# A dense SwiGLU layer whose first three column groups multiply the un-normalised residual

## The chip, the cores and the metric

The kernel runs on one NeuronCore of one Trainium2 chip, as one program in one launch. The metric is the device time of one execution, in microseconds (us); lower is better. The core has five engines with a queue each: TensorE (PE, the matmuls), VectorE (DVE), ScalarE (ACT), GpSimdE (POOL) and SyncE (SP, which here only issues transfers). Work on one engine runs in the order of its queue; engines wait for each other through semaphores. SBUF is the on-chip memory of 128 partitions, PSUM the accumulators that TensorE writes and the other engines read.

## The reference

Two trunk layers over 768 tokens (512 latent, 256 context), width 1024. Each layer adds the output projection of four token mixers to the residual stream, and then a channel mix. Layer 0 has a dense SwiGLU, layer 1 a mixture of experts (MoE). What matters here is the end of layer 0's mixers and its channel mix:

```python
x_lat = x_lat + g1 * (jnp.concatenate([hg_l, rw_l, sw_l, ml_l], axis=-1) @ w_out[l])
h2 = rms_norm(x_lat, norm2_g[l]) * (1.0 + sc2) + sh2          # x * rsqrt(mean(x*x)+eps) * g
x_lat = x_lat + g2 * swiglu(h2, w1, w3, w2)                   # (silu(h2@w1) * (h2@w3)) @ w2
# the context tokens likewise, with csc2, csh2, cg1, cg2 in place of sc2, sh2, g1, g2
```

All of it is float32. The factor rsqrt(mean(x*x)+eps) is one number per token, the scale and shift one number per channel and kind of token (latent or context).

## The kernel before, in words

**Layout.** Activations are stored with channels on the partitions: the residual stream is eight tiles `s.x[m]` of 128 channels x 768 tokens (`xm` in the trace). The tokens are handled in two segments, `SEG`: 512 latent and 256 context ones. A float32 product is made of three matmuls in a reduced format: both factors are split into a rounded part and a remainder (`hi`, `lo`), and `mm3` issues hi x hi (L272), lo x hi (L273) and hi x lo (L274). So a weight column group of 128 columns costs 8 k-tiles x 3 matmuls x 2 segments = 48 matmuls. A weight tile comes by a transfer from SP's queue (`load_split`, L264, `raww`), ScalarE rounds it (L259, `hiw`), VectorE or GpSimdE forms the remainder (L260, `low`).

**End of the mixers.** In `mixers` the output projection runs over m = 0 to 7, one group of 128 output channels each. Behind each product `residual` (L1291, two VectorE instructions) adds it to the stream, and `sumsq` adds the squares of the new tile to `acc` (ScalarE L475, GpSimdE L476; for m = 7 VectorE L476, by segments). m = 7 is multiplied segment by segment (`gemm_last`).

**The norm.** `norm_rs` (L481 to L496) turns `acc` into the tokens' factors: matmuls with a column of ones (L487), square root on ScalarE (L489), reciprocal on VectorE (L490), transposes that spread the factors over the partitions (L492), first for the 512 latent tokens and then for the 256 context tokens. Where a tile `rs` is given they are copied out of PSUM (L495). `norm` (L498 to L512) makes, per k-tile and segment, nt = x * A * rs (VectorE L510), the rounded hhi = nt + shift (ScalarE L511) and the remainder hlo (VectorE L512): 32 VectorE and 16 ScalarE instructions for all eight k-tiles.

**The dense layer.** `ffn` (L1542) loads the first three column groups, (0,0), (0,1) and (1,0) (hidden block f, matrix w1 or w3), then does the norm, then multiplies these three together with k outermost (`gemm_cols`), so that they can follow the norm from k-tile to k-tile. Group (1,1) follows alone; then the hidden blocks go on, two groups each, with Silu on ScalarE (L1567), the product on VectorE (L1568) and a split into `gh`, `gl`. Between (1,1) and (2,0) TensorE makes 16 small transposes for the next layer's modulation (L319, in four PSUM groups, copied out at L320 by ScalarE), and VectorE multiplies it (L456). After each of three passes over the hidden blocks the w2 products are added to the stream. The last pass ends in the input norm of layer 1, which uses the same `norm_rs` with `rs` given.

**What sets the order.** The program is written in the order above; a scheduler then places the instructions on each engine's queue and the tiles in SBUF. Pools on the left side of SBUF are stacked; `fh` (hhi and hlo, 48 KB of each partition), `fg` (gh, gl) and `fw` (weights and scratch of the dense layer) lie on each other; while the output projection runs, its own weights and scratch (`ow`, `ox`) lie on the left as well. A transfer into a tile waits for the last reader of whatever lay there before, and SP's queue holds everything behind it. PSUM holds four tiles `big` of 1024 columns.

Of the kernel before, what the change touches and what calls it, by code (L numbers as in the profile page):

```python
# [11 lines left out]
F32 = mybir.dt.float32  # L12
F32R = mybir.dt.float32r
# [3 lines left out]
AF = mybir.ActivationFunctionType  # L17
OP = mybir.AluOpType
AX = mybir.AxisListType
PSUM = bass.MemoryType.PSUM  # L20
# [3 lines left out]
T = LAT + CTX  # L24
KT = D // 128
# [197 lines left out]
class Ker:  # L223
# [1074 lines left out]
    def mixers(s, l, last, xsrc):  # L1298
# [6 lines left out]
        with ExitStack() as wx, ExitStack() as hx:  # L1305
# [160 lines left out]
            with ExitStack() as ox:  # L1466
# [50 lines left out]
                if last:  # L1517
                    s.moe_open()
                else:
                    s.rest = s.ada_rest(s.fx.enter_context(s.pool("fa", side="right")), lambda: s.big())  # L1520
                with s.pool("ox") as wp, s.pool("po", 1, PSUM) as s.pp:
                    s.nbig = 2 if last else 4
                    if last:
                        s.moe_begin(l, wp)
                    for m in range(KT):
                        if m >= 2:
                            load(m)
                            ps = s.big()
                            s.gemm_last(m, ps, ws[m], act, [x for x in SEG if x[0] < nq])
                            if last:  # L1530
                                s.moe_add(l, m, ps, xos[m], s.ow)
                            else:
                                s.residual(s.mods[l][:, 16:24], m, ps, nq, xos[m])
                        if last:
                            s.moe_x(m, wp)
                        else:
                            s.sumsq(m, nq, wp)
                    if last:
                        s.moe_route(wp)


    def ffn(s, l):  # L1542
        E, V, S = s.E, s.V, s.S
        with s.pool("fh") as hh, s.pool("pf", 1, PSUM) as s.pp:
            hhi = hh.tile([128, KT, T], F32R, name="hhi")
            hlo = hh.tile([128, KT, T], F32R, name="hlo")
            with s.pool("fg") as gp, s.pool("fw") as wp:
                def load(f, u):

# [1 line left out]
                first, early = [(0, 0), (0, 1), (1, 0)], [(1, 1), (2, 0)]  # L1551
                loaded = [load(*x) for x in first]
                s.adaw = lambda: wp.tile([128, KT, 128], F32, name="raww", bufs=4).rearrange("p a b -> p (a b)")
                s.norm(l, s.mod2, 0, 8, P_N2, wp, s.norm_rs(wp, None), hhi, hlo, range(KT))

                def up(cols, loaded=None):
                    c = [(s.big(), w, SEG) for w in loaded or [load(*x) for x in cols]]
                    s.gemm_cols(c, lambda k: (hhi[:, k], hlo[:, k]))
                    return [x[0] for x in c]
                pss = up(first, loaded)  # L1560
                for f0, nf in ((0, 8), (8, 7), (15, 7)):
                    gs = []
                    for f in range(f0, f0 + nf):
                        while len(pss) < 2:
                            pss += up([(f, len(pss))])
                        t = wp.tile([128, T], F32, name="fs", bufs=2)
                        S.activation(t, pss[0][:, :T], AF.Silu)  # L1567
                        V.tensor_mul(t, t, pss[1][:, :T])  # L1568
                        a = gp.tile([128, T], F32R, name=f"gh{f - f0}")
                        c = gp.tile([128, T], F32R, name=f"gl{f - f0}")  # L1570
                        s.split(a, c, t)
                        gs.append((a, c))
                        for _ in range((0 if f == 0 else 1 if f == 8 else 2)):
                            next(s.rest, None)
                        pss = pss[2:]
# [411 lines left out]
```

## Time and profile before

| | |
|---|---|
| median of 3 runs | 2631.07 us (2624.13 to 2632.36) |
| profiled execution | 2628.14 us, its span 2626.2 us, 1.94 us outside |
| TensorE busy | 2406.9 us, 92% of the span; mean granted clock 0.967 |
| VectorE, ScalarE, GpSimdE busy | 1588.0, 1233.2, 478.2 us |
| output projection's last matmul starts | 794.95 us |
| first matmul of the dense layer starts | 804.23 us |
| dense layer's last matmul starts | 1363.38 us |

Times within the span count from its start. A busy share is a mean over very different stretches: TensorE works without a pause in most of the dense layer, and stands still in places around the norms. The granted clock is the share of TensorE's full clock that the chip allowed it in a stretch: 1.00 is 2.4 GHz, 0.50 is 1.2 GHz, and a value between is a stretch with some of both.

### The profile page before, as it was taken

How to read it: one execution, taken by the hardware profiler on the slowest of the kernel's cores; microseconds unless marked ns; L12 is line 12 of the kernel's file. 1: busy time of each engine (PE TensorE's matmuls, PEld its weight loads, DVE VectorE, ACT ScalarE, POOL GpSimd, SP SyncE). 2: the span in 40 equal slices, each digit the busy share in tenths (PEclk: the TensorE clock that was granted, in tenths of full speed). 3: DMA queues.
4: the chain of work that ended last, by engine and by line, in shares of the span. 5: the costliest groups of instructions: out<-in, count | busy, mean ns of one | idle time of the engine just before them, and what ended most of it. 6: DMA issues, size and time to landing. Idle time of an engine off the chain costs nothing. (4 is left out here: it accounts for less than half of the span.)

```text
span 2626.2 us, 46769 instructions
## 1 busy us (share of the span) xinstructions
PE 2406.9 (92%) x18379; PEld 1997.7 (76%) x18379; DVE 1588.0 (60%) x2981; ACT 1233.2 (47%) x2347; POOL 478.2 (18%) x613
## 2 busy tenths in 40 slices
PE   6999889879999999999999997888996999999994
PEld 4889666656587888888888786666674898898993
DVE  5573588877525643443236747877745667767765
ACT  4373356646723211212234644664753565656553
POOL 2010455441011000000020005654112000000002
PEclk9999899999999999999999998999997999999997
DMA  6223222221031533333212130001113888888885
GB/s 247 70 84 111 68 71 84 86 82 57 1 125 47 162 113 121 122 115 117 81 61 72 52 114 13 20 16 56 51 48 120 266 268 276 277 260 264 263 272 178
DMA packets 173061, 322.49 MB, mean 123 GB/s; under 512 B 12033, under 2 KB 100865, under 8 KB 172833
## 3 DMA queue, kind: packets, MB, share of 16 engines
q1 hardware_dynamic: 165776, 293.60, 34.9%
q0 software_dynamic: 6480, 23.73, 2.5%
q8 instruction: 146, 2.39, 0.4%
q10 hardware_dynamic: 576, 2.10, 0.2%
q14 instruction: 83, 0.67, 0.1%
HBM read 295.39 MB, written 22.54 MB: 121 GB/s over the span
## 5 line engine op out<-in xcount | busy, mean ns | idle before, releaser
L272 PE MATMUL big<-hhi,hiw 128*128 128x512 f32 (+1 forms) x1504 | 520.6, 347 | 9.8 <-ACT hhi L511 6.1
L273 PE MATMUL big<-hlo,hiw 128*128 128x512 f32 (+1 forms) x1504 | 522.1, 347 | 2.4 <-DVE hlo L512 2.4
L274 PE MATMUL big<-hhi,low 128*128 128x512 f32 (+1 forms) x1504 | 518.4, 345 | 0.9 <-POOL low L260 0.9
L259 ACT CAST hiw<-raww 128x512 fp32r<-128x512 f32 (+3 forms) x208 | 158.7, 769 | 616.3 <-PE big L273 405.2
L272 PEld LDWEIGHTS big<-hhi,hiw 128*128 128x128 f32 x1504 | 285.9, 190 | 53.7 <-ACT hhi L511 7.6
L273 PEld LDWEIGHTS big<-hlo,hiw 128*128 128x128 f32 x1504 | 285.8, 190 | 40.2 <-DVE hlo L512 3.9
L274 PEld LDWEIGHTS big<-hhi,low 128*128 128x128 f32 x1504 | 285.4, 190 | 38.5 <-issue 1.7
L260 DVE TENSOR_TENSOR lom<-rawm,him 128x1024 fp32r<-128x1024 f32 x176 | 215.2, 1225 | 126.3 <-ACT him L259 124.2
L260 DVE TENSOR_TENSOR low<-raww,hiw 128x512 fp32r<-128x512 f32 (+3 forms) x196 | 172.4, 884 | 185.8 <-ACT hiw L259 185.3
L259 ACT CAST him<-rawm 128x1024 fp32r<-128x1024 f32 x176 | 184.3, 1047 | 149.1 <-PE sml L273 64.0
L272 PE MATMUL sml<-xh,him 128*128 128x256 f32 x528 | 152.1, 288 | 0.0
L273 PE MATMUL sml<-xl,him 128*128 128x256 f32 x528 | 149.7, 284 | 0.0
L274 PE MATMUL sml<-xh,lom 128*128 128x256 f32 x528 | 149.7, 283 | 0.0
L260 DVE TENSOR_TENSOR lov<-rawv,hiv 128x1024 fp32r<-128x1024 f32 x88 | 107.6, 1223 | 40.5 <-ACT hiv L259 40.4
L272 PE MATMUL sml<-him,xh 128*128 128x256 f32 x440 | 127.5, 290 | 0.6 <-DVE xl L260 0.6
L273 PE MATMUL sml<-lom,xh 128*128 128x256 f32 x440 | 125.5, 285 | 0.0
L274 PE MATMUL sml<-him,xl 128*128 128x256 f32 x440 | 125.4, 285 | 0.0
L273 PE MATMUL big<-gl,hiw 128*128 128x512 f32 (+1 forms) x352 | 119.6, 340 | 0.0
L272 PE MATMUL big<-gh,hiw 128*128 128x512 f32 (+1 forms) x352 | 119.1, 338 | 0.0
L274 PE MATMUL big<-gh,low 128*128 128x512 f32 (+1 forms) x352 | 118.3, 336 | 0.0
L259 ACT CAST hiv<-rawv 128x1024 fp32r<-128x1024 f32 x88 | 92.4, 1050 | 54.2 <-PE y L274 43.9
L777 POOL TENSOR_TENSOR Gm<-G,mskf 128x256 f32<-128x256 f32 x120 | 97.2, 815 | 81.2 <-PE a L632 77.5
(557 smaller groups left out, 5568.4 us busy)
## 6 DMA issues: line engine op xcount, KB each, us to landing
rawm<-in_m SPq DMA_DIRECT2D x176, 512.0 KB, 5.0
rawv<-in_m SPq DMA_DIRECT2D x88, 512.0 KB, 5.0
raww<-in_w SPq DMA_DIRECT2D x52, 512.0 KB, 3.7
raww<-in_wadt SPq DMA_DIRECT2D x48, 512.0 KB, 3.5
raww<-in_winc SPq DMA_DIRECT2D x92, 256.0 KB, 2.9
wada<-in_wada SPq DMA_DIRECT2D x16, 1024.0 KB, 6.1
raww<-in_wout SPq DMA_DIRECT2D x16, 512.0 KB, 4.4
raww<-in_w SPq DMA_DIRECT2D x16, 448.0 KB, 3.3
```

The costliest lines, as they stand in the source:

```text
L259: s.S.copy(hi, src)
L260: (eng or s.V).tensor_sub(lo, src, hi)
L272: s.E.matmul(out, ah, bh, start=start, stop=False)
L273: s.E.matmul(out, ah, bl, start=False, stop=False)
L274: s.E.matmul(out, al, bh, start=False, stop=stop)
L777: P.tensor_mul(x, G[:, :, 0, :, 0], s.mskf[:, 1 - d, i][:, None, None].to_broadcast(sh))
```

## The change

The tokens' factors do not depend on the channel, so they can be applied behind a product as well as ahead of it: (x * A * rs + shift) @ W = rs * ((x * A) @ W) + shift @ W. The change uses that for the first three column groups.

- A pool `uh` on the right side of SBUF holds `s.uh`, hi and lo of 8 k-tiles x 770 columns. `norm_scale` computes A and puts the shifts of the two kinds of tokens into columns 768 and 769. `scaled(m)`, called behind each `sumsq`, writes x * A, rounded and remainder: 2 ScalarE (L1562) and 2 VectorE instructions (L1563) for each m.
- `ffn` multiplies the three groups from `s.uh` with segments of 512 and 258 columns; only then come `norm_rs` (into `acc`) and `norm`, which writes the normalised hi and lo over the same tiles. The pool `fh` is gone.
- `normed` multiplies each of the three products by the factors in PSUM (L1584) and copies its two shift columns out (L1586, `nb`). They enter as the bias of the Silu (L1608) and as the addend of the product with w3 (L1610).

```diff
--- before.py
+++ after.py
@@ -1517,6 +1517,11 @@
                 if last:
                     s.moe_open()
                 else:
+
+                    uh = s.fx.enter_context(s.pool("uh", side="right"))
+                    s.uh = [uh.tile([128, KT, T + 2], F32R, name=f"u{n}") for n in "hl"]
+                    s.uA = uh.tile([128, KT, 2], F32, name="uA")
+                    s.norm_scale(s.uA)
                     s.rest = s.ada_rest(s.fx.enter_context(s.pool("fa", side="right")), lambda: s.big())
                 with s.pool("ox") as wp, s.pool("po", 1, PSUM) as s.pp:
                     s.nbig = 2 if last else 4
@@ -1535,15 +1540,32 @@
                             s.moe_x(m, wp)
                         else:
                             s.sumsq(m, nq, wp)
+                            s.scaled(m)
                     if last:
                         s.moe_route(wp)
 
 
+    def norm_scale(s, A):
+
+        V = s.V
+        V.scalar_tensor_tensor(A, s.mod2[:, 8:16], 1.0, s.prm[:, 0, P_N2:P_N2 + 8][:, :, None].to_broadcast([128, KT, 2]),
+                               op0=OP.add, op1=OP.mult)
+        hi, lo = (x[:, :, T:] for x in s.uh)
+        V.tensor_copy(hi, s.mod2[:, :8])
+        V.tensor_sub(lo, s.mod2[:, :8], hi)
+
+    def scaled(s, m):
+
+        hi, lo = (x[:, m] for x in s.uh)
+        for v, (o, n) in enumerate(SEG):
+            c = slice(o, o + n)
+            s.S.activation(hi[:, c], s.x[m][:, c], AF.Copy, scale=s.uA[:, m, v:v + 1])
+            s.V.scalar_tensor_tensor(lo[:, c], s.x[m][:, c], s.uA[:, m, v:v + 1], hi[:, c], op0=OP.mult, op1=OP.subtract)
+
     def ffn(s, l):
         E, V, S = s.E, s.V, s.S
-        with s.pool("fh") as hh, s.pool("pf", 1, PSUM) as s.pp:
-            hhi = hh.tile([128, KT, T], F32R, name="hhi")
-            hlo = hh.tile([128, KT, T], F32R, name="hlo")
+        with s.pool("pf", 1, PSUM) as s.pp:
+            hhi, hlo = s.uh
             with s.pool("fg") as gp, s.pool("fw") as wp:
                 def load(f, u):
 
@@ -1551,21 +1573,43 @@
                 first, early = [(0, 0), (0, 1), (1, 0)], [(1, 1), (2, 0)]
                 loaded = [load(*x) for x in first]
                 s.adaw = lambda: wp.tile([128, KT, 128], F32, name="raww", bufs=4).rearrange("p a b -> p (a b)")
-                s.norm(l, s.mod2, 0, 8, P_N2, wp, s.norm_rs(wp, None), hhi, hlo, range(KT))
+
+                useg = (0, LAT), (LAT, CTX + 2)
+                pss = [s.big() for _ in first]
+                s.gemm_cols([(ps, w, useg) for ps, w in zip(pss, loaded)], lambda k: (hhi[:, k], hlo[:, k]))
+                rs = s.acc
+                s.norm_rs(wp, rs)
+
+                def normed(ps):
+                    V.tensor_mul(ps[:, :T], ps[:, :T], rs)
+                    b = wp.tile([128, 2], F32, name="nb", bufs=3)
+                    V.tensor_copy(b, ps[:, T:T + 2])
+                    return b, ps
+                s.norm(l, s.mod2, 0, 8, P_N2, wp, rs, hhi, hlo, range(KT))
 
                 def up(cols, loaded=None):
                     c = [(s.big(), w, SEG) for w in loaded or [load(*x) for x in cols]]
                     s.gemm_cols(c, lambda k: (hhi[:, k], hlo[:, k]))
-                    return [x[0] for x in c]
-                pss = up(first, loaded)
+                    return [(None, x[0]) for x in c]
+
+                pss = [normed(ps) for ps in pss]
                 for f0, nf in ((0, 8), (8, 7), (15, 7)):
                     gs = []
                     for f in range(f0, f0 + nf):
                         while len(pss) < 2:
                             pss += up([(f, len(pss))])
                         t = wp.tile([128, T], F32, name="fs", bufs=2)
-                        S.activation(t, pss[0][:, :T], AF.Silu)
-                        V.tensor_mul(t, t, pss[1][:, :T])
+                        (b1, x1), (b3, x3) = pss[:2]
+                        if b1 is None:
+                            S.activation(t, x1[:, :T], AF.Silu)
+                        for v, (o, n) in enumerate(SEG):
+                            k = slice(o, o + n)
+                            if b1 is not None:
+                                S.activation(t[:, k], x1[:, k], AF.Silu, bias=b1[:, v:v + 1])
+                            if b3 is not None:
+                                V.scalar_tensor_tensor(t[:, k], x3[:, k], b3[:, v:v + 1], t[:, k], op0=OP.add, op1=OP.mult)
+                        if b3 is None:
+                            V.tensor_mul(t, t, x3[:, :T])
                         a = gp.tile([128, T], F32R, name=f"gh{f - f0}")
                         c = gp.tile([128, T], F32R, name=f"gl{f - f0}")
                         s.split(a, c, t)
```

How the queues stand before and after. Names in the rows: `in_w` are the dense layer's weights, `in_wout` the output projection's, `in_wadt` the next layer's modulation, `xo` the old stream for `residual`. SyncE's queue around the last part of the output projection, before:

```order
L264 DMA raww<-in_wout 128x1024 x2
L264 DMA raww<-in_w 128x1024 x4
L451 DMA raww<-in_wadt 128x1024 x2
L264 DMA raww<-in_w 128x1024
L1481 DMA xo<-in_xT 128x768 x2
L264 DMA raww<-in_wout 128x1024 x2
L1481 DMA xo<-in_xT 128x768
```

And after:

```order
L264 DMA raww<-in_wout 128x1024 x2
L1481 DMA xo<-in_xT 128x768 x2
L264 DMA raww<-in_wout 128x1024 x2
L1481 DMA xo<-in_xT 128x768
L264 DMA raww<-in_wout 128x1024
L1481 DMA xo<-in_xT 128x768
L264 DMA raww<-in_wout 128x1024
L1481 DMA xo<-in_xT 128x768 x2
L264 DMA raww<-in_w 128x1024 x4
L451 DMA raww<-in_wadt 128x1024 x2
```

The first five weight tiles of the dense layer have moved from the middle of the output projection's loads to behind the last of them; the tiles that they fill now lie where the output projection's weights and scratch lie, and the first of the five waits for the last matmul of the projection and the last L476.

TensorE's queue from the last matmul of the output projection, before (`big<-hhi,hiw` behind L492 is the product of the first three groups):

```order
L274 MATMUL big<-hhi,low 128x256
L487 MATMUL big<-cst,acc 128x1 x4
L492 MATMUL big<-cst,rstd_8356 128x128 x4
L487 MATMUL big<-cst,acc 128x1 x2
L492 MATMUL big<-cst,rstd_8365 128x128 x2
L272 MATMUL big<-hhi,hiw 128x512 x3
L273 MATMUL big<-hlo,hiw 128x512
```

And after, from the last two matmuls of the three groups; the first of the 144, `L272 MATMUL big<-uh,hiw 128x512`, now stands directly behind the output projection:

```order
L273 MATMUL big<-ul,hiw 128x258
L274 MATMUL big<-uh,low 128x258
L487 MATMUL big<-cst,acc 128x1 x4
L492 MATMUL big<-cst,rstd_8539 128x128 x4
L487 MATMUL big<-cst,acc 128x1 x2
L492 MATMUL big<-cst,rstd_8549 128x128 x2
L272 MATMUL big<-uh,hiw 128x512
L273 MATMUL big<-ul,hiw 128x512
L274 MATMUL big<-uh,low 128x512
```

The factors' matmuls have moved from ahead of the 144 matmuls of the three groups to between them and group (1,1).

VectorE's queue after the change at the end of the norm (before, nothing stands between the last L512 and the first product L1568 there):

```order
L510 SCALAR_TENSOR_TENSOR nt<-xm_68,nA,acc 128x256
L1584 TENSOR_TENSOR big<-big,acc 128x768
L512 SCALAR_TENSOR_TENSOR ul<-nt,mod_95,uh 128x256
L1586 COPY nb<-big 128x2
L1584 TENSOR_TENSOR big<-big,acc 128x768 x2
L1586 COPY nb<-big 128x2 x2
L260 TENSOR_TENSOR low<-raww,hiw 128x1024
L1610 SCALAR_TENSOR_TENSOR fs<-big,nb,fs 128x512
L1610 SCALAR_TENSOR_TENSOR fs<-big,nb,fs 128x256
```

Behind the norm's last instruction the rest of the three groups' post-processing has come in, ahead of what frees their PSUM tiles. At the end of the dense layer SyncE's queue changes too: ten of the loads of layer 1's projection weights (`in_winc`, 128x512) stood between the last loads of `in_w`, and stand now behind the copies of the last stream tiles (`xd<-xm`).

## Rows read from the trace of the kernel before

**Rows 1.** page, part 1: busy us of each engine

```profile
PE 2406.9 (92%) x18379; PEld 1997.7 (76%) x18379; DVE 1588.0 (60%) x2981; ACT 1233.2 (47%) x2347; POOL 478.2 (18%) x613
```

**Rows 2.** three stretches: length, then busy us per engine, PE clock, DMA share

```profile
797.60:804.20 6.60, 3.83 (x18) 3.29 (x18) 2.14 (x6) 1.27 (x4) 0.00 (x0) 0.54 0.01 1
804.20:808.20 4.00, 3.97 (x11) 3.30 (x12) 4.00 (x9) 2.38 (x5) 0.00 (x0) 0.50 0.00 0
808.20:829.60 21.40, 21.40 (x125) 18.79 (x124) 11.71 (x22) 6.38 (x12) 0.00 (x0) 0.99 0.00 1
```

**Rows 3.** the sum over seven stretches from 853 to 1363 us

```profile
sum 510.00, PE 510.00 PEld 447.03 DVE 206.54 ACT 104.42 POOL 16.67; mean PE 72.86 PEld 63.86 DVE 29.51 ACT 14.92 POOL 2.38
```

**Rows 4.** TensorE in time, 794.9 to 842.7: start, length, line, operation, [idle before]

```profile
794.95 0.28 PE L274 MATMUL big<-hhi,low 128*128 128x256 f32 x1
...
797.69 1.38 PE L487 MATMUL big<-cst,acc 128*128 128x1 f32 x8 [2.45 <-DVE acc L476]
...
804.23 0.80 PE L272 MATMUL big<-hhi,hiw 128*128 128x512 f32 x1 [1.59 <-ACT hhi L511]
...
831.43 0.40 PE L272 MATMUL big<-hhi,hiw 128*128 128x512 f32 x1
...
841.01 1.91 PE L319 MATMUL big<-cst,scp 128*128 128x128 f32 x16
842.67 0.48 PE L272 MATMUL big<-hhi,hiw 128*128 128x512 f32 x1
```

**Rows 5.** VectorE in time, 796.8 to 833

```profile
796.85 1.03 DVE L476 TENSOR_TENSOR acc<-acc,sq 128x512 f32<-128x512 f32 x2 [0.44 <-ACT sq L475]
...
802.68 1.80 DVE L510 SCALAR_TENSOR_TENSOR nt<-xm,nA,big 128x512 f32<-128x512 f32 x3 [0.78 <-PE big L492]
...
820.00 0.48 DVE L512 SCALAR_TENSOR_TENSOR hlo<-nt,mod,hhi 128x256 fp32r<-128x256 f32 x1 [0.58 <-ACT hhi L511]
832.62 0.95 DVE L1568 TENSOR_TENSOR fs<-fs,big 128x768 f32<-128x768 f32 x1 [12.13 <-ACT fs L1567]
```

**Rows 6.** SyncE, ScalarE and VectorE in time: the first FFN weights

```profile
727.55 1.75 SPq L264 DMA_DIRECT2D raww<-in_w  x4
...
731.21 1.05 ACT L259 CAST hiw<-raww 128x1024 fp32r<-128x1024 f32 x1 [3.04 <-DMA raww<-in_w]
...
734.87 1.05 ACT L259 CAST hiw<-raww 128x1024 fp32r<-128x1024 f32 x1 [1.20 <-DMA raww<-in_w]
...
732.28 1.23 DVE L260 TENSOR_TENSOR low<-raww,hiw 128x1024 fp32r<-128x1024 f32 x1 [4.49 <-ACT hiw L259]
```

**Rows 7.** VectorE and TensorE at column m = 2

```profile
742.18 2.20 DVE L1291 SCALAR_TENSOR_TENSOR xm<-sc,mod,xo 128x512 f32<-128x512 f32 x4 [5.00 <-PE sc L274]
744.28 2.36 DVE L260 TENSOR_TENSOR low<-raww,hiw 128x1024 fp32r<-128x1024 f32 x2
...
744.52 0.47 PE L272 MATMUL big<-hhi,hiw 128*128 128x512 f32 x1 [2.02 <-DVE xm L1291]
```

**Rows 8.** ScalarE behind the first three columns

```profile
830.48 1.28 ACT L1567 ACT_TABLE_LOAD   x1
...
841.64 1.07 ACT L320 COPY cb<-big 128x512 f32<-128x512 f32 x2 [3.94 <-PE big L319]
```

**Rows 9.** the boundary to layer 1: TensorE, VectorE, SyncE, casts, transfers

```profile
1366.12 1.02 PE L487 MATMUL big<-cst,acc 128*128 128x1 f32 x8 [2.45 <-DVE acc L476]
...
1371.01 0.80 PE L272 MATMUL big<-hhi,hiw 128*128 128x512 f32 x1
...
1369.02 0.75 DVE L510 SCALAR_TENSOR_TENSOR rwr<-xm,nA,rwvt 128x512 f32<-128x512 f32 x1 [1.37 <-ACT rwvt L495]
...
1307.38 8.86 SPq L264 DMA_DIRECT2D raww<-in_winc  x5
...
L259 ACT CAST hiw<-raww 128x512 fp32r<-128x512 f32 x6 | 3.7, 618 | 7.7 <-PE big L273 7.6
...
raww<-in_winc SPq DMA_DIRECT2D x10, 256.0 KB, 3.9
```

## The prediction

> **What bounds the kernel now.** I read the page first, then TensorE's time line around the dense layer, then the other engines' time lines over the same stretch, and last the boundary to layer 1. The page gives TensorE 92% of the span [rows 1], so the question is where TensorE stands still and whether the change fills or makes such places. The table of stretches answers for the body of the dense layer: from 853 to 1363 us TensorE is busy for all of the 510 us [rows 3]. Nothing lost or won ahead of that stretch can be given back or eaten in it; a microsecond at its start is a microsecond at its end.
>
> The place that the change aims at is the norm. The output projection's last matmul starts at 794.95, the first one of the dense layer at 804.23: a hole of 9.0 us in which only the small matmuls of the factors run [rows 4]. The clock follows: 0.54 in the hole, 0.50 for the 4.0 us behind it, then 0.99 [rows 2]. Four us at half speed do two us of work, so the hole costs some 11 us in all. The three groups then run from 804.23 to 831.43, that is 27.2 us, or 25.2 at full clock; 8.4 us for one group. VectorE's norm lies beside them: its 32 instructions take from 802.68 to 820.48, 17.8 us [rows 5], and are through 11 us before the product is. That cover matters most below.
>
> **The change part by part.**
>
> *Weights.* Before, the first weights were issued at 727.55 and rounded from 731.21 on, the third at 734.87 [rows 6], 70 us before use. In the new order of SyncE their loads stand behind the last load of the output projection, into memory that it uses until its last square is added. That addition (L476) ends at 797.88 [rows 5]. It also comes a little later: at m = 2 VectorE's remainder of a weight now stands behind two more instructions (L1563), for which I take half of the 2.20 us of four L1291 of the same sizes, 1.1 us, and TensorE waits at that place as it is [rows 7]; bounds 0 and 2.2. So the loads go out at 799.0. By the intervals of before (3.66 us to the first cast, 7.32 to the third [rows 6]) the first cast starts at 802.6, the first matmul at 803.7; the third remainder starts 1.07 behind its cast, takes 1.23, and is ready at 808.6. With k outermost the three groups need all three weights for their first k-tile. If that waits for the weights alone, the other seven k-tiles (7/8 of 25.2 = 22.0) end at 831; if the clock is at half, the first k-tile takes 6.3 us and they end at 832. I take 832.0 against 831.43: the hole is not filled, but changes its cause, from the norm to the weights. Term: +0.6, bounds -1 and +3. The 32 new instructions of `scaled` otherwise lie beside TensorE's output projection, where VectorE and ScalarE wait for products; the two extra columns of 72 matmuls are under 0.1 us.
>
> *The norm behind the product.* Call the product's end G. In TensorE's new order the factors' matmuls come behind the 144, and group (1,1) behind those. `norm` overwrites what the 144 read, and (1,1) reads what it writes, so the whole pass now stands between them. The factors with `rs` given are in the trace, at the boundary to layer 1: first L487 at 1366.12, first L510 at 1369.02 [rows 9], 2.9 us. Then VectorE's pass, 17.8 us [rows 5], with one L1584 inside it that I price as L1568, 0.95 us for 768 columns out of PSUM [rows 5], and the reciprocal and copy of the second segment, 0.5 us. The last L512 ends at G + 22.2, and (1,1) just behind it, at G + 22.6. Before, (1,1) ended 9.6 us behind the product (841.01 - 831.43 [rows 4]). That is +13.0. Where before three groups of matmuls (27 us) covered the pass, one group of 8.4 us is left to do it.
>
> *What frees PSUM.* The transposes L319 need the tiles of the three products. Behind the last L512 VectorE has two L1584 (1.9), three small copies (0.4), one weight remainder (1.23 [rows 6]) and two L1610 (1.1, as L1291 [rows 7]): 4.6 us. Then the last group of transposes (a quarter of 1.91 [rows 4]) and its copy (half of 1.07 [rows 8]) and (2,0) can start: G + 27.8, where before it started at 842.67, G + 11.2. The whole term from G to (2,0) is +16.6, the 13.0 within it. Bounds: 13 if VectorE's instructions run closer together without an operand in PSUM and the tail lies beside the transposes, 19 if ScalarE's Silus with bias and their table load (1.28 [rows 8]) come last in the tail.
>
> *Clock.* No row shows TensorE behind such a sparse stretch, but the rows of the hole do: half speed after some 7 us that were half idle [rows 2]. In (1,1) half speed would cost little, since a k-tile takes 2.1 us at half and the pass gives one each 2.2. Behind the 5 us of the tail, (2,0) would lose 2 us in its first 4. I take +1.5; bounds 0 and 4.
>
> *The boundary to layer 1.* Ten loads of layer 1's weights went out before the dense layer's end, five of them at 1307.38 [rows 9]. Now they stand behind the last copies of the stream and come in only after the layer's last matmul. A load takes 3.9 us at the median, a cast 0.62 [rows 9]. In ScalarE's and VectorE's new order two or three casts and remainders, and two table loads for the square root, get in between L489, L495 and L510, on a chain that is already the path from 1366.12 to 1371.01 [rows 9]. Two casts and the first table load ahead of the first L510 are 2.5 us, the second table load delays the context tokens further: +3.0; bounds 0 (all of it beside waits) and 5 (two table loads and four casts in a row).
>
> On those table loads a rule speaks for more. The row shows 1.28 us, and ScalarE starts its next instruction 0.01 us behind it, at 831.77 after 830.48 + 1.28 [rows 8]. The Trainium skill (ScalarE: Activation LUTs, "What ACT_TABLE_LOAD costs") adds a drain to each switch and comes to about 2.66 us; by it the boundary would be some 2.8 us dearer. This trace shows no such gap behind the load, so the sum keeps the row.
>
> **The sum.** 0.6 + 16.6 + 1.5 + 3.0 = +21.7 us, against a profiled execution of 2628.14 (span 2626.2 and 1.94 around it): 2649.8. The median of the runs shown is 2.9 above that execution, so by the median it is 2652.8. I predict 2651. The bounds of all terms together are +12 and +31.
>
> **The rivals.**
>
> *A: the product closes the hole.* If the first weights are there (the transfers wait for less than I read from the order, or land beside the last additions), the product starts at 795.2 at full clock and ends at 820.4, 11 us earlier. For it: the order does put the 144 matmuls straight behind the projection, and 76 us before use was time enough so far. Against: SyncE's order, and the reuse of memory. The pass behind it is still paid: -11 + 16.6 + 1.5 makes +7, less or more with the boundary (0 to 3): 2635 to 2641, at the edge of no change.
>
> *B, the other side: the factors leave the path for good.* The mechanism would be that group (1,1) does not wait for the whole pass because VectorE's work for it is done beside TensorE's, as now. Its place is the stretch between the product and (2,0); it decides at 2.2 us for a k-tile on VectorE against 1.05 on TensorE at full clock. If the pass were ahead of TensorE and the hole closed too, the gain is the whole 11 us, minus about 3 us of chain: 2620 to 2623. Against: 17.8 us of work on one engine, and 8.4 us of matmuls left to hide it.
>
> *C: a larger loss.* TensorE's clock stays at half through the sparse 28 us and beyond. The row that speaks for it is the 0.54 and 0.50 around 801 [rows 2]. A k-tile of (1,1) then takes a little more than the pass gives, the transposes and the first groups behind run at half, and the boundary costs its upper bound: +6 for the clock in place of 1.5, +5 in place of 3, +3 for the weights: +31 us, 2660 to 2664. The Trainium skill (TensorE: Matmul & The Clock Gate, "A second HAM failure mode: psum-queue depth-cycling") tells of a kernel in which short idle times between groups of matmuls made the clock swing between its two levels; here (1,1) would have such pauses in front of each k-tile. What the trace of before has of it is the one hole at 797.6.
>
> *D: no effect where it aims, and none elsewhere.* If the pass behind the product lay beside other TensorE work, the time would be unchanged, about 2631 to 2634. TensorE's queue is in order, and nothing stands there that could run meanwhile, so this needs the order not to be what runs.
>
> **How the numbers follow.** The forecast (+12 to +27) has a chance of 0.74, C 0.09, A 0.10, D 0.03, B 0.04. What a measurement of this kernel can tell from no change is about 0.3%, 7.9 us, so up to 2639 counts as the same. A lies half across that edge: faster 0.04 (B), same 0.10 (D, most of A, and a sliver of the forecast's low end), slower 0.86. The range leaves out B, D, half of A and the far end of C: 2637 to 2663.
>
> **What would show it.** Weights: the first `big<-uh,hiw` matmul near 804, with TensorE waiting for ScalarE's cast or VectorE's remainder, and `raww<-in_w` issued near 799. The norm: L487 directly behind the product near 832; (1,1) drawn out over about 20 us with waits for ScalarE's or VectorE's output; (2,0) near 860. Clock: a stretch of 0.5 behind 832, and full clock soon after (2,0). Boundary: layer 1's first `big<-hhi,hiw` about 8 us, not 5, behind its first L487. I would be wrong if the first weights are loaded long before 795, if (1,1) follows the product within 5 us at its old speed, or if TensorE shows idle time in the 510 us that are full now.

## The result, and the profile after

The changed kernel takes 2653.63 us (median of 6 runs, 2650.56 to 2657.03), the kernel before 2630.11 (6 runs, 2624.13 to 2632.36). The ratio is 1.0095, with a 95% interval of 1.0079 to 1.0111: slower by 25 us, 21 to 29 (the two medians differ by 23.5). The forecast was 2651, from a sum of +21.7.

The profiled execution took 2654.09 us with a span of 2652.3, 26.1 more than before. TensorE's time line of the changed kernel, as in [rows 4]:

```profile
799.64 0.28 PE L274 MATMUL big<-hhi,low 128*128 128x256 f32 x1
...
807.77 0.77 PE L272 MATMUL big<-uh,hiw 128*128 128x512 f32 x1 [7.85 <-issue]
...
835.88 0.95 PE L487 MATMUL big<-cst,acc 128*128 128x1 f32 x8
837.40 0.65 PE L492 MATMUL big<-cst,rstd 128*128 128x128 f32 x4 [0.57 <-DVE rstd L490]
838.73 0.61 PE L487 MATMUL big<-cst,acc 128*128 128x1 f32 x4 [0.68 <-ACT acc L495]
840.39 0.69 PE L492 MATMUL big<-cst,rstd 128*128 128x128 f32 x2 [1.06 <-DVE rstd L490]
841.68 0.77 PE L272 MATMUL big<-uh,hiw 128*128 128x512 f32 x1 [0.61 <-DVE acc L495]
...
859.72 0.65 PE L319 MATMUL big<-cst,scp 128*128 128x128 f32 x4 [1.15 <-ACT fs L1608]
861.16 2.82 PE L319 MATMUL big<-cst,scp 128*128 128x128 f32 x12 [0.79 <-ACT fs L1608]
863.63 0.75 PE L272 MATMUL big<-uh,hiw 128*128 128x512 f32 x1
```

The hole behind the output projection is still there (799.64 to 807.77), the three groups follow, and at 835.88 the factors begin, where before group (1,1) began at once. (1,1) starts at 841.68, and (2,0) at 863.63: 27.75 us behind the product's end and not 11.24 [rows 4]. What TensorE waited for from 790 to 870 (engine, line, by whom: us in total, times, longest; `issue` means that the profile shows nothing it waited for):

```profile
PE big L272 <- issue: 7.9, 1, 7.9
PE big L273 <- DVE ul L512: 2.4, 4, 0.9
PE big L319 <- ACT fs L1608: 1.9, 2, 1.1
PE big L492 <- DVE rstd L490: 1.6, 2, 1.1
```

VectorE, SyncE and ScalarE, as in [rows 5, 6, 8]: the last addition, the loads right behind it, the first casts, and the norm pass between the product and (1,1)'s end.

```profile
801.54 1.03 DVE L476 TENSOR_TENSOR acc<-acc,sq 128x512 f32<-128x512 f32 x2 [0.44 <-ACT sq L475]
...
838.71 1.55 DVE L510 SCALAR_TENSOR_TENSOR nt<-xm,nA,acc 128x512 f32<-128x512 f32 x1 [1.36 <-ACT acc L495]
...
857.54 0.47 DVE L512 SCALAR_TENSOR_TENSOR ul<-nt,mod,uh 128x256 fp32r<-128x256 f32 x1
...
802.69 1.75 SPq L264 DMA_DIRECT2D raww<-in_w  x4
...
806.63 2.14 ACT L259 CAST hiw<-raww 128x1024 fp32r<-128x1024 f32 x2 [3.88 <-issue]
...
857.32 1.28 ACT L1608 ACT_TABLE_LOAD   x1
858.62 1.05 ACT L1608 ACTIVATE fs<-big,nb 128x512 f32<-128x512 f32 x2
```

The granted clock over the sparse stretch, as in [rows 2]:

```profile
840.00:845.00 5.00, 3.67 (x9) 2.27 (x10) 4.87 (x11) 3.25 (x5) 0.00 (x0) 0.53 0.37 118
845.00:850.00 5.00, 4.76 (x19) 3.46 (x18) 5.00 (x11) 3.23 (x6) 0.00 (x0) 0.78 0.00 0
850.00:856.00 6.00, 3.93 (x16) 2.45 (x16) 6.00 (x12) 3.48 (x6) 0.00 (x0) 1.00 0.00 0
862.00:866.00 4.00, 4.00 (x22) 3.68 (x21) 3.69 (x6) 3.13 (x5) 0.00 (x0) 0.72 0.41 131
```

It is at half where (1,1) begins (0.53), and back to full (1.00 from 850 to 856) while TensorE still waits in front of each k-tile; behind the tail, around the start of (2,0), it falls once more for a moment (0.72). The boundary to layer 1, as in [rows 9]:

```profile
1388.46 1.02 PE L487 MATMUL big<-cst,acc 128*128 128x1 f32 x8 [2.45 <-DVE acc L476]
...
1396.09 1.63 PE L272 MATMUL big<-hhi,hiw 128*128 128x512 f32 x3
...
1393.56 0.74 DVE L510 SCALAR_TENSOR_TENSOR rwr<-xm,nA,rwvt 128x512 f32<-128x512 f32 x1
...
1390.31 1.28 ACT L921 ACT_TABLE_LOAD   x1
1391.61 0.20 ACT L921 ACTIVATE lb<-lb 128x4 f32<-128x4 f32 x1
...
1393.86 1.28 ACT L489 ACT_TABLE_LOAD   x1
...
1386.04 0.81 SPq L264 DMA_DIRECT2D raww<-in_winc  x2
...
1387.38 13.01 SPq L264 DMA_DIRECT2D raww<-in_winc  x8
```

The loads of `in_winc` start 2.4 us ahead of the first L487, where the first of them started some 60 us ahead of it before; casts and two table loads come in on ScalarE, and the first L510 is 5.1 us behind the first L487 (2.9 before), the first matmul of layer 1 7.6 us (4.9).

### The profile page after: what moved, and what is told of

Read it like the earlier page. It is cut to its first block, busy times and chain, and to the rows that moved or that the text cites. A ratio compares the mean times of both kernels' runs of the same rounds, so it can differ in the third digit from the quotient of the medians.

```text
span 2652.3 us, 46837 instructions
## 1 busy us (share of the span) xinstructions
PE 2416.6 (91%) x18379; PEld 1999.4 (75%) x18379; DVE 1610.5 (61%) x3008; ACT 1248.2 (47%) x2370; POOL 480.6 (18%) x613
## 5 line engine op out<-in xcount | busy, mean ns | idle before, releaser
L272 PE MATMUL big<-hhi,hiw 128*128 128x512 f32 (+1 forms) x800 | 280.6, 352 | 7.3 <-ACT hhi L511 3.5
L273 PE MATMUL big<-hlo,hiw 128*128 128x512 f32 (+1 forms) x800 | 282.0, 353 | 3.1 <-DVE hlo L512 3.1
L274 PE MATMUL big<-hhi,low 128*128 128x512 f32 (+1 forms) x800 | 280.5, 351 | 1.4 <-DVE low L260 1.4
L272 PE MATMUL big<-uh,hiw 128*128 128x512 f32 x704 | 240.9, 342 | 9.0 <-issue 7.9
L273 PE MATMUL big<-ul,hiw 128*128 128x512 f32 x704 | 240.5, 342 | 2.7 <-DVE ul L512 2.4
L274 PE MATMUL big<-uh,low 128*128 128x512 f32 x704 | 239.1, 340 | 0.0
L272 PEld LDWEIGHTS big<-hhi,hiw 128*128 128x128 f32 x800 | 151.7, 190 | 35.3 <-ACT hhi L511 5.6
L273 PEld LDWEIGHTS big<-hlo,hiw 128*128 128x128 f32 x800 | 151.5, 189 | 28.1 <-DVE hlo L512 5.2
L272 PEld LDWEIGHTS big<-uh,hiw 128*128 128x128 f32 x704 | 134.4, 191 | 26.8 <-issue 8.0
L272 PE MATMUL sml<-xh,him 128*128 128x256 f32 x528 | 151.9, 288 | 0.0
L273 PEld LDWEIGHTS big<-ul,hiw 128*128 128x128 f32 x704 | 134.2, 191 | 20.0 <-DVE ul L512 4.5
L260 DVE TENSOR_TENSOR lov<-rawv,hiv 128x1024 fp32r<-128x1024 f32 x88 | 107.6, 1222 | 35.1 <-ACT hiv L259 35.0
L272 PE MATMUL sml<-him,xh 128*128 128x256 f32 x440 | 127.1, 289 | 0.6 <-DVE xl L260 0.6
```

The lines of the kernel that those rows point to most:

```text
L260: (eng or s.V).tensor_sub(lo, src, hi)
L272: s.E.matmul(out, ah, bh, start=start, stop=False)
L273: s.E.matmul(out, ah, bl, start=False, stop=False)
L274: s.E.matmul(out, al, bh, start=False, stop=stop)
```

## The experiments

Times are medians with the ratio to the kernel before, measured beside it on the same chip. The stretches in the table at the end of this section are read from each run's trace.

**1. The factors ahead of the product.**

```diff
-                s.gemm_cols([(ps, w, useg) for ps, w in zip(pss, loaded)], lambda k: (hhi[:, k], hlo[:, k]))
                 rs = s.acc
                 s.norm_rs(wp, rs)
+                s.gemm_cols([(ps, w, useg) for ps, w in zip(pss, loaded)], lambda k: (hhi[:, k], hlo[:, k]))
```

> The changed kernel with one thing moved: the tokens' factors (L487 to L495) are computed ahead of the three groups' product again, so that the in-place norm can follow the product's k-tiles. Theory (the loss is the norm pass standing between the product and group (1,1)): the hole ahead of the product stays, its first matmul near 808, because the weights still come late; the product ends near 836 as in the changed kernel; (2,0) starts 11 to 14 us behind the product's end and not 28; the time falls by 13 to 16 us, to about 2638 to 2640, and is still some 9 us above the kernel before. Rival (the moved memory is the loss, not the order): the time stays near 2653, with the 28 us as they were.

Measured: 2636.78 us, ratio 1.0032 (1.0015 to 1.0048), 17 us less than the changed kernel, a little below the expected range. TensorE, and ScalarE's first two casts:

```profile
796.00 0.28 PE L274 MATMUL big<-hhi,low 128*128 128x256 f32 x1
798.74 1.02 PE L487 MATMUL big<-cst,acc 128*128 128x1 f32 x8 [2.45 <-DVE acc L476]
...
803.56 0.69 PE L492 MATMUL big<-cst,rstd 128*128 128x128 f32 x2 [0.55 <-DVE rstd L490]
804.30 0.80 PE L272 MATMUL big<-uh,hiw 128*128 128x512 f32 x1
...
843.17 1.91 PE L319 MATMUL big<-cst,scp 128*128 128x128 f32 x16
844.83 0.48 PE L272 MATMUL big<-uh,hiw 128*128 128x512 f32 x1
...
803.21 1.98 ACT L259 CAST hiw<-raww 128x1024 fp32r<-128x1024 f32 x2
```

The product starts 8.3 us behind the projection, as late as in the changed kernel, although the factors' whole chain now stands in that hole. The last L492 (803.56 + 0.69) and the first cast end within 0.1 us of each other, so either alone would hold the product about as long. (2,0) comes 48.8 us behind the projection's end, where the changed kernel needs 64.0. (1,1) now starts right behind the product, at 833.45, and (2,0) 11.4 us later. The order was the loss, as the theory had it: 15.3 of the 17 us came back between the product's first matmul and (2,0). The rival of the moved memory alone falls: its memory is where it was.

**2. The raw weights early.**

```diff
-            with s.pool("fg") as gp, s.pool("fw") as wp:
+            with s.pool("fg") as gp, s.pool("fw") as wp, s.pool("fr", side="right") as rp:
...
-                s.adaw = lambda: wp.tile(
+                s.adaw = lambda: rp.tile(
...
+                        sq = [wp.tile([128, T], F32, name="sq")] * 2
...
-                            s.sumsq(m, nq, wp)
+                            s.sumsq(m, nq, sq)
```

(Both calls of `load_split` in the dense layer take `rp` for the raw tile as well.)

> The changed kernel with the raw weight tiles of the dense layer in a pool of their own on the right side of SBUF, in memory that the output projection does not use (its square scratch is one tile in place of two for that), so that their loads go out in the middle of the projection as before. Rounding still has to wait for the projection's end, since the rounded tiles lie in its memory. Theory: the first FFN matmul starts 1.5 to 3 us behind the projection's end in place of 8.1, the product ends 5 to 7 us earlier, the stretch from there to (2,0) is 27 to 28 us as in the changed kernel, layer 1's boundary as in the changed kernel: 2646 to 2649. Rival (the moved memory is the whole loss): the time comes near that of the kernel before, 2630 to 2636. Rival (the hole is the chain of the last addition, not the weights): no change.

Measured: 2647.47 us, ratio 1.0078 (1.005 to 1.0107). The loads went out at 728.51 and the hole shrank from 8.1 to 4.15 us, a little over the expected 1.5 to 3: the three casts stand behind the last tile's squares and scaling on ScalarE (801.81, where the projection's last matmul started at 798.79). The stretch behind the product is the changed kernel's (27.6 us). Both rivals fall: the time is far from that of the kernel before, and the hole shrank although the chain of the last addition was not touched.

```profile
799.96 0.94 ACT L475 ACTIVATE sq<-xm 128x512 f32<-128x512 f32 x2 [4.76 <-DVE xm L1291]
800.80 1.11 ACT L1564 ACTIVATE uh<-xm,uA 128x512 fp32r<-128x512 f32 x2
801.81 2.93 ACT L259 CAST hiw<-raww 128x1024 fp32r<-128x1024 f32 x3
...
802.94 0.77 PE L272 MATMUL big<-uh,hiw 128*128 128x512 f32 x1 [3.87 <-issue]
```

**3. No norm pass at all.**

```diff
-                s.norm(l, s.mod2, 0, 8, P_N2, wp, rs, hhi, hlo, range(KT))
...
-                    c = [(s.big(), w, SEG) for w in loaded or [load(*x) for x in cols]]
+                    c = [(s.big(), w, useg) for w in loaded or [load(*x) for x in cols]]
...
-                    return [(None, x[0]) for x in c]
+                    return [normed(x[0]) for x in c]
```

> The changed kernel without the norm pass: all 44 column groups multiply the un-normalised residual, and each product gets its factors and its shift behind it (one L1584 and one L1586 more for each of the other 41 groups, and two L1610 in place of one product). Theory: behind the three groups' product only the factors' chain is left ahead of (1,1), about 6 us, then its 8.4 us and the transposes: (2,0) 16 to 18 us behind the product in place of 28, the time 10 to 12 us lower, 2641 to 2644; VectorE's 41 x 1.3 = 53 us more lie beside TensorE, which is full from there on. Rival (VectorE becomes the bound in the body of the layer): TensorE shows waits for VectorE between the groups there, and the time does not fall, or rises.

Measured: 2645.86 us, ratio 1.0075 (1.0047 to 1.0103), 2 us above the expected range. The place does what was expected: factors at 831.26, (2,0) at 848.09, 16.8 us and not 27.75. TensorE shows no wait in the body of the layer, so VectorE's additional work is hidden; but the body is 4.2 us longer than before (524.96 and 520.71 us). Of these 1.1 us are there in every trace with the residual's tiles on the right side (last section). The rest goes with the products of this run: 96 matmuls take 17.01 us and not 16.85, which is 3.3 ns more for each of the 48 that have two columns more. At the mean of 0.46 ns per column (16.80 us for 48 x 768 columns) two columns would be 0.9 ns; why they cost more was not tried. The rival of VectorE, waits between the groups, falls.

**4 and 7. The kernel before with the hidden activations at the bottom.**

```diff
-        with s.pool("fh") as hh, s.pool("pf", 1, PSUM) as s.pp:
+        with s.pool("fg") as gp, s.pool("fh") as hh, s.pool("pf", 1, PSUM) as s.pp:
...
-            with s.pool("fg") as gp, s.pool("fw") as wp:
+            with s.pool("fw") as wp:
```

> The kernel before with one thing changed: the tiles of the hidden activations (gh, gl) lie at the bottom of the left side and the normalised residual above them, the other way round than before. This is where gh and gl lie in the changed kernel. Nothing else moves around the first three groups. Theory: the loads of layer 1's first weights wait for the dense layer's last matmul, and the boundary (first L487 to layer 1's first matmul) goes from 4.9 to about 7.6 us, as in the changed kernel: +2.5 to +3, 2633. Rival (the boundary got longer by the later order of the casts alone, or for another reason than memory): no change, 2630.

> The kernel before with the hidden activations at the bottom once more (the fourth run): there the trace showed the boundary 2.7 us longer, and the time was 9.9 us above before, more than its own trace adds up to (3.3 us). Theory (the boundary and the waits for weights behind it are all that changes, the rest was the spread of single executions): +2 to +5. Rival (the layout costs some 10 us, in a place which that trace did not catch): +8 to +12 again, and the trace shows the place.

Measured: 2638.16 us, ratio 1.0043 (1.003 to 1.0056), then 2635.39, ratio 1.0025 (1.0014 to 1.0036). Both traces have the boundary as the changed kernel has it. The second one's:

```profile
1362.64 1.02 PE L487 MATMUL big<-cst,acc 128*128 128x1 f32 x8 [2.46 <-DVE acc L476]
...
1367.55 1.01 PE L487 MATMUL big<-cst,acc 128*128 128x1 f32 x4 [2.67 <-ACT rwvt L495]
...
1370.26 1.65 PE L272 MATMUL big<-hhi,hiw 128*128 128x512 f32 x3
...
1316.96 37.07 SPq L1962 DMA_DIRECT2D xd<-xm  x6
1360.22 0.81 SPq L264 DMA_DIRECT2D raww<-in_winc  x2
...
1361.55 13.02 SPq L264 DMA_DIRECT2D raww<-in_winc  x8
...
PE big L273 <- DVE low L260: 1.6, 2, 1.2
```

From the dense layer's last matmul to layer 1's first are 10.35 us in both (7.63 before), and the layout alone does it: no other edit is in this kernel. But the time rose by 9.9 and 6.7 us, more than these 2.7. Some of the rest is behind the boundary: the later loads also bring waits of TensorE for a weight remainder, in this trace at 1523 and 1530 (the last line). All nine traces with gh and gl low have such waits, 1.2 to 1.8 us in all, and neither trace of the kernel before has one. The stretch from layer 1's first matmul on is 4 us longer in both traces, but that is not shown to be the layout's: with the same layout it is as short as before in the changed kernel and in runs 2 and 5, and long in runs 1, 3, 6 and 9, and the six traces that have it long all came to m = 2 early (table). So by their medians the layout costs these two kernels 4 to 7 us more than the boundary shows, run 7 between the two ranges expected; where, and how much of that the changed kernel pays, stays open.

**5. The losses mended together.** Early raw weights as in run 2, and:

```diff
-                s.gemm_cols([(ps, w, useg) for ps, w in zip(pss, loaded)], lambda k: (hhi[:, k], hlo[:, k]))
-                rs = s.acc
-                s.norm_rs(wp, rs)
+                gc = lambda ks: s.gemm_cols([(ps, w, useg) for ps, w in zip(pss, loaded)], lambda k: (hhi[:, k], hlo[:, k]), ks)
+                gc(range(0, 1))
...
+                gc(range(1, 3))
...
+                gc(range(3, KT))
...
-                            s.scaled(m)
+                            if m >= 3:
+                                s.scaled(m - 3)
+                            if m == KT - 1:
+                                for j in (KT - 3, KT - 2, m):
+                                    s.scaled(j)
```

(Behind the first k-tile stand the matmuls with ones, the square roots and the reciprocals, behind the third the transposes and the copies.)

> The changed kernel with its three losses around the product mended: raw weights early (as in the second run), the factors' matmuls behind the product's first k-tile and their transposes behind its third, so that neither stands in front of TensorE and the in-place norm runs beside the product, and the scaled tiles of m three columns later in the program, so that the remainder of a weight comes first on VectorE at m = 2. Theory: m = 2 to the projection's end 50 to 51.5 us (before 50.4, changed 53.4), then a hole of 3 to 4 us (9.3 and 8.1), product and (1,1) as in the first run or better, (2,0) about 43 us behind the projection's end (before 47.7, changed 64.0); the boundary to layer 1 stays 2.7 us longer. Sum against the kernel before: 0 - 4.5 + 2.7 = about -2, range -5 to +3, 2624 to 2631 where before is 2628. Rival (the product with un-normalised rows costs something that no row has shown, in its matmuls or by the clock): +5 to +9 as in the first run.

Measured: 2634.92 us, ratio 1.0021 (1.0009 to 1.0033), 6 us above the kernel before and 4 above the range that the theory gave: as much as the rival had it. The trace does not bear the rival out, though: from the projection's end to (2,0) this kernel is 1.3 us shorter than the kernel before, and 3.5 us are lost at the boundary (11.2 and 7.6) and 1.1 in the body; the projection's 1.5 us more stand in run 8 too, in the kernel before. By the medians the 6 us are no more than the 6.7 of run 7, which has nothing of the change but the layout. Still, projection to (2,0) took 46.4 us and not 43: the transposes stood behind the third k-tile, so VectorE idled for 6.6 us ahead of the first L510 at 810.20, and the pass ended at 832, behind the product. No version here beats the kernel before.

**6. The scaled tiles later in the program.** The part of the edit above that moves `scaled`, alone.

> The changed kernel with only this: the scaled tiles of m are written in the program three columns later, so that VectorE makes the weight's remainder for m = 2 before the scaled tiles, as the kernel before does. Theory: the 3.0 us that the output projection got longer from m = 2 on (50.4 to 53.4) are that remainder's wait (1.4 us) and the half clock behind it; the stretch comes back to 50.4 to 51.5 and the time falls by 2 to 3 us, to about 2650. Rival (the additional work of ScalarE and VectorE as such slows the projection, wherever it stands): the stretch stays above 53.

Measured: 2650.21 us, ratio 1.0081 (1.0063 to 1.01). VectorE makes both remainders at 740.37, right behind the residual, and TensorE's wait for them at m = 2 is gone; the stretch from m = 2 to the projection's end is 51.84 us, a little above the expected 51.5. That is inside what traces without scaled tiles show (50.43 to 51.99), and 1.4 to 2.7 below those that have them at m = 2 (53.27 to 54.54). The rival falls: the work is still done, and costs nothing there that this spread would show. The other half of the theory falls too: without the wait the granted clock is at half all the same (0.50 from 741.2 to 744.4).

**8. The kernel before once more.** Unchanged.

> The kernel before, unchanged, measured as if it were another: both theories expect 1.000 in the ratio, within 0.2%. Its trace tells how far the stretches that no edit touches (from the start to m = 2; from layer 1's first matmul to the end) move from one execution to the next, which the accounts of the other runs need: by the six traces so far 740 to 746 us to m = 2.

Measured: 2627.99 us, ratio 0.9996 (0.9985 to 1.0008). Its trace is 5 us longer than that of the first execution; m = 2 to the projection's end (+1.6), the boundary (+1.3) and the start and the end of the program moved. The two on which the verdict on the norm rests did not: projection to (2,0) 47.97 (47.72), body 520.71 (520.71).

**9. Longer rows for the residual's tiles.**

```diff
-                    s.uh = [uh.tile([128, KT, T + 2], F32R, name=f"u{n}") for n in "hl"]
+                    s.uh = [uh.tile([128, KT, T + 8], F32R, name=f"u{n}") for n in "hl"]
...
-        hi, lo = (x[:, :, T:] for x in s.uh)
+        hi, lo = (x[:, :, T:T + 2] for x in s.uh)
```

> The changed kernel with rows of 776 elements in place of 770 for the residual's two tiles, all else the same. In every run with these tiles, 96 matmuls of the body (two column groups) take 16.85 us, in every run without them 16.80: 1.1 us over the layer. Theory (the row length: 770 elements put the rows of the k-tiles at odd offsets): 16.80 again. Rival (it is where the tiles lie, or their having been written in place, and not the row length): 16.85 as before. The time itself, some 1 us less or the same, can't tell them apart.

Measured once: 2652.24 us (before beside it 2628.04). 96 matmuls took 16.88 us: not the row length. The theory falls.

The stretches of all traces, in us: start to m = 2; m = 2 to the projection's last matmul; from there to the first matmul of the dense layer; from there to (2,0); (2,0) to the layer's last matmul; from there to layer 1's first; from there to the last matmul of the program.

| run | to m=2 | projection | hole | to (2,0) | body | boundary | layer 1 |
|---|---|---|---|---|---|---|---|
| before | 744.5 | 50.4 | 9.3 | 38.4 | 520.7 | 7.6 | 1217.9 |
| 8 before again | 745.4 | 52.0 | 8.9 | 39.0 | 520.7 | 8.9 | 1217.1 |
| changed | 746.2 | 53.4 | 8.1 | 55.9 | 522.1 | 10.4 | 1217.5 |
| 1 factors first | 741.5 | 54.5 | 8.3 | 40.5 | 521.8 | 10.4 | 1221.4 |
| 2 weights early | 745.5 | 53.3 | 4.1 | 55.9 | 522.2 | 10.3 | 1217.4 |
| 3 no pass | 740.2 | 54.3 | 8.3 | 45.3 | 525.0 | 11.2 | 1222.1 |
| 4, 7 gh, gl low | 739.6 | 51.8 | 9.3, 9.1 | 38.5 | 520.7 | 10.4 | 1221.8 |
| 5 mended | 740.2 | 52.0 | 4.2 | 42.3 | 521.8 | 11.2 | 1217.9 |
| 6 scaled later | 740.6 | 51.8 | 8.2 | 56.0 | 522.0 | 10.4 | 1220.4 |
| 9 rows of 776 | 740.3 | 54.4 | 7.9 | 55.1 | 523.5 | 10.4 | 1221.3 |

## Why the prediction was right

**The norm behind the product: right in size, and in mechanism up to the tail.** Forecast +16.6 from the product's end to (2,0), measured 27.75 - 11.24 = +16.5. Up to the pass's end its parts came as worked out: the first L510 2.8 us behind the first L487 (838.71 and 835.88), the last L512 ending at 858.01, 22.1 us behind the product's end (22.2 in the forecast). The tail took the forecast's 5.6 us, but by another path. VectorE's chain was through with its second L1610 at 862.20. TensorE's two waits there, 1.15 and 0.79 us, were for ScalarE's Silus behind their table load, which the forecast had in its upper bound alone, and the last twelve of the transposes then ran at half clock:

```profile
861.10:863.60 2.50, 2.44 (x12) 2.44 (x13) 2.50 (x5) 1.50 (x4) 0.00 (x0) 0.50 0.56 164
```

They took 2.5 us, where all sixteen took 1.9 before [rows 4]. That the tail's size agrees is luck. Run 1 takes this loss alone away and gets 17 us back, and run 3, which has no pass, 11 us at that place. Four traces with the changed order have the stretch from the first matmul to (2,0) within 1 us (55.1 to 56.0), so the term is the change's and no accident of one execution.

**The weights: right in mechanism, too small in the sum.** The loads went out 0.1 us behind the last L476, the first matmul came 5.1 us after that, and the three groups took 28.1 us (28.3 by the forecast's own times). The step that failed is the price of the stop at m = 2: I took 1.1 us, with a bound of 2.2, for the two instructions ahead of the remainder, and nothing for the clock; the projection got 3.0 us longer in this trace. The two instructions took the 1.1 us, TensorE waited 1.4 us for the remainder and then worked at half clock for some 3 us (clock rows as in [rows 2]):

```profile
745.99 1.14 DVE L1563 SCALAR_TENSOR_TENSOR ul<-xm,uA,uh 128x512 fp32r<-128x512 f32 x2
747.05 1.22 DVE L260 TENSOR_TENSOR low<-raww,hiw 128x1024 fp32r<-128x1024 f32 x1
...
748.32 0.80 PE L274 MATMUL big<-hhi,low 128*128 128x512 f32 x1 [1.40 <-DVE low L260]
...
748.30:751.40 3.10, 3.08 (x10) 2.70 (x11) 3.10 (x3) 0.97 (x2) 1.65 (x1) 0.50 0.66 233
...
746.80:750.30 3.50, 3.50 (x13) 2.99 (x12) 0.76 (x1) 0.00 (x0) 2.44 (x1) 0.54 0.80 276
```

The last row is the kernel before in run 8: the half clock stands there too, without that wait, and in every other trace but the first one of the kernel before. So only the wait is shown to be the change's; against run 6 its price is 1.4 to 2.7 us, by how long the half clock lasts. With it the product ended 4.4 us later than before in the trace, not 0.6; 1.7 of these are from ahead of m = 2, where the program is the same, and the two traces of the kernel before differ by 0.9 there. The two extra columns of the 72 matmuls, under 0.1 us in the forecast, would be 0.24 us by run 3's price.

**The clock: too large for this trace, and nearly right in sum by another cause.** I took +1.5 for (2,0)'s start at half clock. In the trace the body is 1.4 us longer; but runs 1 and 5, which have no sparse stretch, have it 1.1 us longer as well, so the clock has only some 0.3 us of it. By the same reckoning it has 0.2 to 0.5 us in runs 2 and 6, and 1.2 us in run 9. Another part of the clock's price fell on the transposes, within the term above. That (1,1) at half clock would cost little was right. Rival C, the clock at half through the whole stretch and beyond, did not come: here the clock was back at 1.00 from 850 to 856 with waits in front of each k-tile. But it does not stay there in every execution. Run 9, with the same work in this stretch:

```profile
841.00:850.00 9.00, 6.60 (x27) 4.18 (x28) 9.00 (x18) 4.93 (x8) 0.00 (x0) 1.00 0.00 0
...
851.00:857.60 6.60, 5.41 (x22) 4.06 (x21) 6.60 (x12) 5.18 (x9) 0.00 (x0) 0.50 0.21 63
```

There the clock fell to half again while (1,1) was still fed k-tile by k-tile, and (2,0) ran its first 2.7 us at half. The rule of the Trainium skill that stood beside rival C (TensorE: Matmul & The Clock Gate, "A second HAM failure mode: psum-queue depth-cycling") tells of a swinging clock in such a pattern. Run 9 agrees with it, at a price within the forecast's bounds of 0 and 4.

**The boundary: right at the place.** Forecast +3.0, measured +2.7 (10.36 and 7.63), and runs 4 and 7 have it from the layout alone. The other execution of the kernel before shows 8.9, so +1.5 to +2.7. The table loads cost what the row said: 1390.31 + 1.28 is 1391.59, and the next instruction starts at 1391.61. The drain that the Trainium skill states (ScalarE: Activation LUTs, "What ACT_TABLE_LOAD costs"), by which an estimate of this term would have been 5.8, does not show here either. What the forecast did not have is what the late loads do behind the boundary: the waits for weight remainders, and what the medians of runs 4 and 7 show beyond their traces.

**The rivals.** A (the product closes the hole) and B (the factors leave the path) did not come: the weights came late for the reason read from the order, and only (1,1) lay beside the pass. D fell with B. The sum of the terms, 21.7, and the measured 23.5 agree better than the terms do, and that is in part luck: the stop at m = 2 was too small, the clock too large, the body's slower matmuls (below) were not foreseen, and of the trace's 26.1 us 2.7 lie ahead of m = 2 and behind layer 1's first matmul, in stretches that move by as much without an edit.

## What to carry to other kernels

A pass that costs nothing does so because of something long beside it: before moving that cover, look for what it hides. Here 17.8 us of norm lay beside 27 us of matmuls, and moving the matmuls ahead of the norm laid the pass open. A tile that goes away moves its neighbours: the first place to look is which early loads now wait for a tile that is still being read. And a gain in one stretch of a single trace is worth only as much as that stretch repeats from one execution to the next.

## What was not expected

The column groups of the body run at 16.85 us for 96 matmuls in the traces with the residual's tiles on the right side (run 3, with its two more columns, apart), and 16.80 in the four without them, from the second pair of groups on and with no wait: 1.1 us over the layer. The products with w2, which read other tiles, take the same time in all (184.6 us). It is not the row length (run 9: 16.88). Whether it is the place of the tiles was not tried.

Stretches that no edit touches move by several us between executions: start to m = 2 from 739.6 to 746.2, layer 1 from 1217 to 1222, while the body of the dense layer repeats within 0.01 us in four traces.
